# Feature-major GEMMs in split float32: one 512-column product for the weights' high part in place of two of 256

## Chip, cores and metric

The kernel runs on one core of one Trainium2 chip. What counts is the device time of one execution, in microseconds (us).

## The reference

One layer of a bidirectional trunk on 256 tokens of 2048 features, in float32. Every sub-layer has a norm ahead of it and a plain residual add behind it. Cut to what matters:

```python
u = rmsnorm(h, mix_norm)
z, xbc, dt = split(u @ w_in)                     # 2048 -> 4096 + 6144 + 128
xs, B, C = split(silu(dwconv(xbc, 4 taps)))      # 4096 + 1024 + 1024
y = ssd_scan(xs, dt, A, B, C) + flipped scan + xs * d_skip
h = h + (rmsnorm(y * silu(z)) * norm_g) @ w_out  # 4096 -> 2048
q = rmsnorm(h) @ wq;  k, v = split(rmsnorm(mem) @ wkv)
h = h + (softmax(q @ k.T / sqrt(512)) @ v) @ wo  # 4 heads of 512
gate, val = split(rmsnorm(h) @ w_up)             # 2048 -> 2 x 5632
h = h + (silu(dwconv(gate, 3 taps)) * val) @ w_down
return rmsnorm(h) * final_norm
```

## The kernel before

**Split operands.** Each float32 operand of a GEMM is split into a high and a low part of type float32r, and a product is the sum of three: high by high, high by low, low by high. An activation unit holds four tiles of 128 features by 256 tokens, with its high and low parts side by side (`new_unit`). Weights come by DMA as raw tiles of 512 KB into a ring of five (`load_weights`, L119). ScalarE casts a tile to `w_hi` (L106), VectorE subtracts to get `w_lo` (L107); each of these rings has four buffers.

**Three forms of GEMM.** `gemm_feat` (L132), the narrow form here, puts features on the partitions. For each k tile and feature tile it issues three matmuls of 256 columns (L152 to L154), and four feature tiles share one PSUM slot `psg` of two banks. `gemm_feat_wide` (L157), the wide form, is used by the FFN's up projection alone. The high part of the weights meets both parts of the activation in one matmul of 512 columns (L169), the low part meets the high one in 256 columns (L171). A feature tile then takes a whole bank, so that a slot holds two, and its halves are added at the end: a copy on ScalarE (L173) and an add on VectorE (L174). `gemm_tok` (L176) puts tokens on the partitions and stays as it is. There are two slots `psg` and four banks `psm`.

**The SSD stage** goes through eight groups. `project(g)` gives four feature tiles of x and one each of B and C (`bc`); `conv_silu` (L354) multiplies the PSUM bank by 1/rms into a tile `cv_s` (two buffers), then applies the taps into `xs` (two buffers) or `bc`. `project_z(g)` gives `sz` (one buffer). `scan_group(g)` turns x to token-major, works out the decays on ScalarE and VectorE, multiplies by `sz` (L460), and splits the result into a unit (`split_scaled`, L101 and L102). The loop has project(g + 1) ahead of z(g) and scan(g), so that the products of the next group run on TensorE while the scan runs on the other engines:

```python
nxt = project(0)
for g in range(GROUPS):
    cur = nxt
    if g + 1 < GROUPS:
        nxt = project(g + 1)
    sz = project_z(g)
    scan_group(g, *cur, sz)
```

**Behind it**, `residual_units` (L476) adds w_out's and wo's output to the residual stream and splits it again; `query` and `key` split their banks into high and low parts; values, the attention products and the down projection are in the other forms.

**Order.** Tiles wait for buffers of their pool. A planner at build time, with a cost model of its own, fixes the order of instructions on each engine; the engines run in that order, with semaphores between them.

Of the kernel before, what the change touches and what calls it, by code (L numbers as in the profile page):

```python
# [36 lines left out]
def kernel(  # L37
# [28 lines left out]
    def psum_g():  # L66
        """two banks"""
        return sb(ps_g, [P, 2, 512], "psg")
# [16 lines left out]
    # tri[:, 0, l] = 1 where l >= m, tri[:, 1, l] = 1 where l <= m  # L85
# [8 lines left out]
    def new_unit():  # L94
        """4 feature tiles of an operand: high part, low part, and both side by side"""
        both = sb(unit_pool, [P, 4, 2, T], "unit", F32R)
        return both[:, :, 0, :], both[:, :, 1, :], both
# [34 lines left out]
    def gemm_feat(units, wv, cols, k_first=0, first_raw=None):  # L132
        """features on the partitions: banks of two 128-feature tiles by 256 tokens"""
# [23 lines left out]
    def gemm_feat_wide(units, wv, c0, dst):  # L157
        """dst [P, 2, T] = two 128-feature tiles; the high part of the weights meets both parts of the
        operand in one product, so each tile has a bank whose halves add up to it"""
        nk = 4 * len(units)  # L160
        ps = psum_g()
        for k0 in range(0, nk, 4):
            hi, lo = load_weights(wv, k0, [(c0, 2 * P)])
            for kk in range(4):
                kt = k0 + kk
                unit = units[kt // 4]
                for ft in range(2):
                    fs = slice(ft * P, (ft + 1) * P)
                    nc.tensor.matmul(ps[:, ft, :], hi[:, kk, fs], unit[2][:, kt % 4].rearrange("p s t -> p (s t)"),  # L169
                                     start=(kt == 0), stop=False, skip_group_check=True)  # L170
                    nc.tensor.matmul(ps[:, ft, :T], lo[:, kk, fs], unit[0][:, kt % 4, :], start=False,  # L171
                                     stop=(kt == nk - 1), skip_group_check=True)
        nc.scalar.copy(out=dst, in_=ps[:, :, T:])  # L173
        nc.vector.tensor_tensor(out=dst, in0=ps[:, :, :T], in1=dst, op=ALU.add)  # L174

    def gemm_tok(units, wv, c0, k_first=0):  # L176
        """tokens on the partitions: two banks of 128 tokens by 512 features"""
# [23 lines left out]
    def add_square(pool, acc, src2, first):  # L201
        """src2: [P, 2, T]"""
# [7 lines left out]
    def rsqrt_mean(pool, dst, total, n, tags=("rs_v", "rs_s")):  # L210
        """dst = (total / n + eps) ** -0.5: a square root from the table, then one Heron step"""
# [25 lines left out]
    w_in_v = kview(w_in)  # L237
    units_mix = [new_unit() for _ in range(4)]
    with tc.tile_pool(name="xin", bufs=1) as xin:
# [32 lines left out]
        # the column of 1/rms as a row on every partition  # L272
# [12 lines left out]
    with tc.tile_pool(name="ssd", bufs=1) as ssd:  # L285
        acc_y = sb(ssd, [P, 2, T], "acc_y")

# [10 lines left out]
        # log1p(ex) = ln(w) * ex / (w - 1) with w = 1 + ex, and ex itself where w == 1  # L298
# [32 lines left out]
        # decay to the end of the chunk times dt: forward for chunk 0, backward for chunk 1  # L331
# [12 lines left out]
        # exp(cum) where a state comes in: forward rows in chunk 1, backward rows in chunk 0  # L344
# [9 lines left out]
        def conv_silu(banks, f0s, dst):  # L354
            """centred conv of 4 taps over the tokens, bias, silu; two feature tiles per bank"""
            for b, bank in enumerate(banks):
                s = sb(ssd, [P, 2, T], "cv_s", bufs=2)
                nc.vector.tensor_tensor(out=s, in0=two(bank), in1=rows2(r_mix), op=ALU.mult)
                a = dst[:, 2 * b:2 * b + 2, :]
                for j in range(2):  # L360
                    f = f0s[2 * b + j]
                    w = lambda t: pcol("conv_w", f * 4 + t)
                    nc.scalar.activation(out=a[:, j, :], in_=s[:, j, :], func=AF.Identity, scale=w(2), bias=pcol("conv_b", f))
                    for tap, off in ((0, 2), (1, 1)):
                        nc.vector.scalar_tensor_tensor(out=a[:, j, off:], in0=s[:, j, :T - off], scalar=w(tap),
                                                       in1=a[:, j, off:], op0=ALU.mult, op1=ALU.add)
                    nc.vector.scalar_tensor_tensor(out=a[:, j, :T - 1], in0=s[:, j, 1:], scalar=w(3),
                                                   in1=a[:, j, :T - 1], op0=ALU.mult, op1=ALU.add)
                nc.scalar.activation(out=a, in_=a, func=AF.Silu)

        def project(g):
            xs = sb(ssd, [P, 4, T], "xs", bufs=2)
            conv_silu(gemm_feat(units_mix, w_in_v, [(INNER + g * 512, 512)]), [g * 4 + j for j in range(4)], xs)
            bc = sb(ssd, [P, 2, T], "bc", bufs=2)
            conv_silu(gemm_feat(units_mix, w_in_v, [(2 * INNER + g * P, P), (2 * INNER + 1024 + g * P, P)]),
# [3 lines left out]
        def project_z(g):  # L379
            sz = sb(ssd, [P, 4, T], "sz")  # L380
            for b, bank in enumerate(gemm_feat(units_mix, w_in_v, [(g * 512, 512)])):
                nc.vector.tensor_tensor(out=sz[:, 2 * b:2 * b + 2, :], in0=two(bank), in1=rows2(r_mix), op=ALU.mult)
                nc.scalar.activation(out=sz[:, 2 * b:2 * b + 2, :], in_=sz[:, 2 * b:2 * b + 2, :], func=AF.Silu)
# [5 lines left out]
        def scan_group(g, xs, bc, sz):  # L389
# [5 lines left out]
            # token-major x and B  # L395
# [15 lines left out]
            # state that leaves chunk 0 forwards, and the one that leaves chunk 1 backwards  # L411
# [5 lines left out]
            for c in range(2):  # L417
# [8 lines left out]
                # of the two exponents the one of the direction that reaches l from m is <= 0, the other >= 0  # L426
# [14 lines left out]
                # what the incoming state gives, before its decay  # L441
# [34 lines left out]
    def residual_units(pool, hT, banks, u, gname, acc_t, r=None):  # L476
        unit = new_unit()
        for b, bank in enumerate(banks):
            hv = hT[:, u * 4 + 2 * b:u * 4 + 2 * b + 2, :]
            if r is None:  # L480
                nc.vector.tensor_tensor(out=hv, in0=two(bank), in1=hv, op=ALU.add)
            else:
                t = sb(pool, [P, 2, T], "res_t", bufs=2)
                nc.vector.tensor_tensor(out=t, in0=two(bank), in1=rows2(r), op=ALU.mult)
# [35 lines left out]
    with tc.tile_pool(name="res", bufs=1) as res:  # L520
# [4 lines left out]
        with tc.tile_pool(name="att", bufs=1) as att:  # L525
# [4 lines left out]
            for u in range(4):  # L530
                banks = gemm_feat(units_y, w_out_v, [(u * 512, 512)])
                units_xa.append(residual_units(att, hT, banks, u, "g_xa", acc_h, r_ssd))
# [7 lines left out]
            # 1/rms of the queries' tokens as columns: it goes into the scale of the softmax  # L540
# [14 lines left out]

            def query(hd):
                return split_banks(pair("q", [P, 4, T]), gemm_feat(units_xa, wq_v, [(hd * 512, 512)]))

            def key(hd):
                return split_banks(pair("k", [P, 4, T]), gemm_feat(units_mem, wkv_v, [(hd * 512, 512)]))  # L560
# [7 lines left out]
            def three(out_ap, lhsT, rhs, first, last):  # L568
                """one product of operands in two parts each; lhsT, rhs: (hi, lo)"""
# [56 lines left out]
            for u in range(4):  # L626
                banks = gemm_feat(units_o, wo_v, [(u * 512, 512)])
                units_ffn.append(residual_units(att, hT, banks, u, "g_ffn", acc_f))
            inv_rms(att, acc_f, r_ffn, D)

# [126 lines left out]
```

## Time and profile before

| | us |
|---|---|
| median of 3 runs | 1872.16 |
| lowest and highest | 1871.01 and 1872.17 |
| span of the profiled execution, from its first to its last instruction | 1870.4 |
| TensorE busy (share of the span) | 1851.4 (99%) |
| VectorE busy | 1246.3 (67%) |
| ScalarE busy | 1007.2 (54%) |

All rows come from the one profiled execution. PE is TensorE's matmuls, PEld its weight loads, DVE VectorE, ACT ScalarE, SP the engine that issues most DMAs. Matmuls are pipelined and their ends are modelled; the distance from one start to the next is what a matmul costs in a stream.

### The profile page before, as it was taken

The page shows a single profiled execution, that of the slowest core. Times are in us where ns is not written, and L with a number is a line of the kernel's source. Part 1 is how long each engine was busy: PE and PEld are TensorE (multiplying, and loading weights), DVE is VectorE, ACT ScalarE, POOL GpSimd, SP SyncE. Part 2 cuts the span into 40 slices and gives each one's busy share as a digit, 9 for nine tenths or more (in the row PEclk, how much of TensorE's full clock was granted, in tenths as well). Part 3 has the DMA queues.
Part 4 walks back from the last instruction along what each step waited for, and adds up shares of the span by engine and source line. Part 5 has one row for each costly group of instructions (what it writes and reads, how often), then busy time and mean ns, then how long its engine had stood idle before and what let it go on. Part 6 is the DMA issues. An engine that isn't in the chain of part 4 may idle for free.

```text
span 1870.4 us, 31851 instructions
## 1 busy us (share of the span) xinstructions
PE 1851.4 (99%) x12845; PEld 1715.6 (92%) x12845; DVE 1246.3 (67%) x1764; ACT 1007.2 (54%) x1434; POOL 2.3 (0%) x11
## 2 busy tenths in 40 slices
PE   8999999999999999999999999999999999999997
PEld 8999999999999999999999998888888888888886
DVE  7778878988887756554454557666664556666654
ACT  6666767766675544444444446555553345555443
POOL 0000000000000000000000000000000000000000
PEclk9999999999999999999999999999999999999999
DMA  8667666766756655555555556566655565656553
GB/s 288 197 201 214 205 197 195 220 199 183 224 183 223 230 188 181 181 161 178 171 178 172 165 182 202 180 189 188 189 191 194 195 192 185 189 184 189 188 195 113
DMA packets 256947, 359.06 MB, mean 192 GB/s; under 512 B 11616, under 2 KB 145120, under 8 KB 256288
## 3 DMA queue, kind: packets, MB, share of 16 engines
q1 hardware_dynamic: 256720, 356.76, 60.8%
q8 instruction: 100, 1.64, 0.4%
q14 instruction: 47, 0.39, 0.1%
q0 software_dynamic: 80, 0.28, 0.0%
HBM read 352.60 MB, written 4.39 MB: 191 GB/s over the span
## 4 chain that ended last, share of the span: by engine, by line
PE 99%; DMA 0%; DVE 0%; ACT 0%; SPq 0%; issue 0%; DVEq 0%
PE psg L169 18%; PE psg L154 17%; PE psg L152 16%; PE psg L153 16%; PE psg L171 9%; PE psm L190 6%; PE psm L191 6%; PE psm L189 6%; PE psm L449 1%; PE psm L444 1%; PE psm L415 1%; PE psm L572 0%; PE psm L570 0%; PE psm L571 0%; DMA x<-in_x_dram 0%; PE psm L401 0%
## 5 line engine op out<-in xcount | busy, mean ns | idle before, releaser
L107 DVE TENSOR_TENSOR w_lo<-raw,w_hi 128x1024 fp32r<-128x1024 f32 x618 | 753.4, 1223 | 518.4 <-ACT w_hi L106 515.7
L106 ACT CAST w_hi<-raw 128x1024 fp32r<-128x1024 f32 x618 | 645.1, 1048 | 697.7 <-PE psg L153 255.0
L154 PE MATMUL psg<-unit,w_lo 128*128 128x256 f32 x2576 | 733.4, 285 | 0.0
L152 PE MATMUL psg<-unit,w_hi 128*128 128x256 f32 x2576 | 731.6, 284 | 0.0
L153 PE MATMUL psg<-unit,w_hi 128*128 128x256 f32 x2576 | 730.3, 284 | 0.0
L154 PEld LDWEIGHTS psg<-unit,w_lo 128*128 128x128 f32 x2576 | 494.3, 192 | 3.4 <-issue 3.1
L152 PEld LDWEIGHTS psg<-unit,w_hi 128*128 128x128 f32 x2576 | 494.4, 192 | 1.7 <-issue 1.7
L153 PEld LDWEIGHTS psg<-unit,w_hi 128*128 128x128 f32 x2576 | 494.5, 192 | 0.3 <-issue 0.2
L169 PE MATMUL psg<-unit,w_hi 128*128 128x512 f32 x1408 | 493.5, 396 | 0.0
L171 PE MATMUL psg<-unit,w_lo 128*128 128x256 f32 x1408 | 393.2, 279 | 0.0
L169 PEld LDWEIGHTS psg<-unit,w_hi 128*128 128x128 f32 x1408 | 264.3, 188 | 63.6
L171 PEld LDWEIGHTS psg<-unit,w_lo 128*128 128x128 f32 x1408 | 265.2, 188 | 0.1
L189 PE MATMUL psm<-w_hi,unit 128*128 128x512 f32 x480 | 186.8, 389 | 0.0
L190 PE MATMUL psm<-w_lo,unit 128*128 128x512 f32 x480 | 186.8, 389 | 0.0
L191 PE MATMUL psm<-w_hi,unit 128*128 128x512 f32 x480 | 186.8, 389 | 0.0
L189 PEld LDWEIGHTS psm<-w_hi,unit 128*128 128x128 f32 x480 | 90.1, 188 | 18.8
L190 PEld LDWEIGHTS psm<-w_lo,unit 128*128 128x128 f32 x480 | 90.1, 188 | 18.6
L191 PEld LDWEIGHTS psm<-w_hi,unit 128*128 128x128 f32 x480 | 90.1, 188 | 18.5
L431 ACT ACTIVATE r<-r,ncum_tok 128x128 f32<-128x128 f32 x128 | 39.4, 390 | 57.7 <-DMA r<-cum_d 55.1
L432 DVE SCALAR_TENSOR_TENSOR r<-r,ncum_tok 128x128 f32<-128x128 f32 x128 | 36.9, 347 | 17.1 <-ACT r L431 17.1
L437 ACT ACTIVATE t<-cb,dt_tok 128x128 f32<-128x128 f32 x128 | 39.1, 388 | 0.7 <-DVE cb L424 0.2
L438 DVE SCALAR_TENSOR_TENSOR t<-cb,dt_tok,t 128x128 f32<-128x128 f32 x128 | 36.5, 348 | 3.3 <-ACT t L437 3.3
(218 smaller groups left out, 1044.7 us busy)
## 6 DMA issues: line engine op xcount, KB each, us to landing
raw<-in_w_up_dram SPq DMA_DIRECT2D x176, 512.0 KB, 3.6
raw<-in_w_in_dram SPq DMA_DIRECT2D x130, 512.0 KB, 4.6
raw<-in_w_down_dram SPq DMA_DIRECT2D x88, 512.0 KB, 3.6
raw<-in_w_out_dram SPq DMA_DIRECT2D x64, 512.0 KB, 4.3
raw<-in_wkv_dram SPq DMA_DIRECT2D x64, 512.0 KB, 3.7
raw<-in_w_in_dram SPq DMA_DIRECT2D x64, 256.0 KB, 4.5
r<-cum_d SPq DMA_DIRECT2D x16, 1024.0 KB, 6.3
raw<-in_wq_dram SPq DMA_DIRECT2D x32, 512.0 KB, 3.6
```

What stands on the lines that cost most here:

```text
L106: nc.scalar.copy(out=hi, in_=src)
L107: nc.vector.tensor_tensor(out=lo, in0=src, in1=hi.bitcast(F32), op=ALU.subtract)
L152: nc.tensor.matmul(dst, wh, uh, start=first, stop=False, skip_group_check=True)
L153: nc.tensor.matmul(dst, wh, ul, start=False, stop=False, skip_group_check=True)
L154: nc.tensor.matmul(dst, wl, uh, start=False, stop=last, skip_group_check=True)
L169: nc.tensor.matmul(ps[:, ft, :], hi[:, kk, fs], unit[2][:, kt % 4].rearrange("p s t -> p (s t)"), start=(kt == 0), stop=False, skip_group_ ...
L171: nc.tensor.matmul(ps[:, ft, :T], lo[:, kk, fs], unit[0][:, kt % 4, :], start=False, stop=(kt == nk - 1), skip_group_check=True)
L189: nc.tensor.matmul(banks[tt], uh, hi[:, kk, :], start=(kt == 0), stop=False)
L190: nc.tensor.matmul(banks[tt], uh, lo[:, kk, :], start=False, stop=False)
L191: nc.tensor.matmul(banks[tt], ul, hi[:, kk, :], start=False, stop=(kt == nk - 1))
L431: nc.scalar.activation(out=t1[:, h, :], in_=t1[:, h, :], func=AF.Identity, bias=ncum_tok[:, c, hf:hf + 1])
L437: nc.scalar.activation(out=t2[:, h, :], in_=cb[:, 1, :], func=AF.Copy, scale=dt_tok[:, c, hb:hb + 1])
```

## The change

`gemm_feat_wide` takes lists of columns, as `gemm_feat` does, and returns its PSUM slot; `add_halves` does the copy and the add. All callers of `gemm_feat` but the one for dt now go through 256 columns at a time with the wide form: `project`, `project_z`, `residual_units` (w_out and wo), `query` and `key`. Where nothing is multiplied in between (wo), the two halves are added to the residual stream one after the other.

```diff
-    def gemm_feat_wide(units, wv, c0, dst):
+    def gemm_feat_wide(units, wv, cols):
         nk = 4 * len(units)
         ps = psum_g()
         for k0 in range(0, nk, 4):
-            hi, lo = load_weights(wv, k0, [(c0, 2 * P)])
+            hi, lo = load_weights(wv, k0, cols)
...
+        return ps
+
+    def add_halves(dst, ps):
         nc.scalar.copy(out=dst, in_=ps[:, :, T:])
         nc.vector.tensor_tensor(out=dst, in0=ps[:, :, :T], in1=dst, op=ALU.add)
...
-        def conv_silu(banks, f0s, dst):
-            for b, bank in enumerate(banks):
-                s = sb(ssd, [P, 2, T], "cv_s", bufs=2)
-                nc.vector.tensor_tensor(out=s, in0=two(bank), in1=rows2(r_mix), op=ALU.mult)
...
+        def conv_silu(ps, f0s, a):
+            s = sb(ssd, [P, 2, T], "cv_s", bufs=2)
+            add_halves(s, ps)
+            nc.vector.tensor_tensor(out=s, in0=s, in1=rows2(r_mix), op=ALU.mult)
...
         def project(g):
             xs = sb(ssd, [P, 4, T], "xs", bufs=2)
-            conv_silu(gemm_feat(units_mix, w_in_v, [(INNER + g * 512, 512)]), [g * 4 + j for j in range(4)], xs)
+            for b in range(2):
+                conv_silu(gemm_feat_wide(units_mix, w_in_v, [(INNER + g * 512 + b * 256, 256)]),
+                          [g * 4 + 2 * b, g * 4 + 2 * b + 1], xs[:, 2 * b:2 * b + 2, :])
             bc = sb(ssd, [P, 2, T], "bc", bufs=2)
-            conv_silu(gemm_feat(units_mix, w_in_v, [(2 * INNER + g * P, P), (2 * INNER + 1024 + g * P, P)]),
+            conv_silu(gemm_feat_wide(units_mix, w_in_v, [(2 * INNER + g * P, P), (2 * INNER + 1024 + g * P, P)]),
                       [32 + g, 40 + g], bc)
...
         def project_z(g):
             sz = sb(ssd, [P, 4, T], "sz")
-            for b, bank in enumerate(gemm_feat(units_mix, w_in_v, [(g * 512, 512)])):
-                nc.vector.tensor_tensor(out=sz[:, 2 * b:2 * b + 2, :], in0=two(bank), in1=rows2(r_mix), op=ALU.mult)
-                nc.scalar.activation(out=sz[:, 2 * b:2 * b + 2, :], in_=sz[:, 2 * b:2 * b + 2, :], func=AF.Silu)
+            for b in range(2):
+                z = sz[:, 2 * b:2 * b + 2, :]
+                add_halves(z, gemm_feat_wide(units_mix, w_in_v, [(g * 512 + b * 256, 256)]))
+                nc.vector.tensor_tensor(out=z, in0=z, in1=rows2(r_mix), op=ALU.mult)
+                nc.scalar.activation(out=z, in_=z, func=AF.Silu)
...
-    def residual_units(pool, hT, banks, u, gname, acc_t, r=None):
+    def residual_units(pool, hT, units, wv, u, gname, acc_t, r=None):
         unit = new_unit()
-        for b, bank in enumerate(banks):
+        for b in range(2):
+            ps = gemm_feat_wide(units, wv, [(u * 512 + b * 256, 256)])
             hv = hT[:, u * 4 + 2 * b:u * 4 + 2 * b + 2, :]
             if r is None:
-                nc.vector.tensor_tensor(out=hv, in0=two(bank), in1=hv, op=ALU.add)
+                nc.vector.tensor_tensor(out=hv, in0=ps[:, :, T:], in1=hv, op=ALU.add)
+                nc.vector.tensor_tensor(out=hv, in0=ps[:, :, :T], in1=hv, op=ALU.add)
             else:
                 t = sb(pool, [P, 2, T], "res_t", bufs=2)
-                nc.vector.tensor_tensor(out=t, in0=two(bank), in1=rows2(r), op=ALU.mult)
+                add_halves(t, ps)
+                nc.vector.tensor_tensor(out=t, in0=t, in1=rows2(r), op=ALU.mult)
...
+            def split_wide(dst, units, wv, c0):
+                for b in range(2):
+                    t = sb(att, [P, 2, T], "res_t", bufs=2)
+                    add_halves(t, gemm_feat_wide(units, wv, [(c0 + b * 256, 256)]))
+                    split_plain(dst[0][:, 2 * b:2 * b + 2, :], dst[1][:, 2 * b:2 * b + 2, :], t)
+                return dst
...
             def query(hd):
-                return split_banks(pair("q", [P, 4, T]), gemm_feat(units_xa, wq_v, [(hd * 512, 512)]))
+                return split_wide(pair("q", [P, 4, T]), units_xa, wq_v, hd * 512)
...
             def key(hd):
-                return split_banks(pair("k", [P, 4, T]), gemm_feat(units_mem, wkv_v, [(hd * 512, 512)]))
+                return split_wide(pair("k", [P, 4, T]), units_mem, wkv_v, hd * 512)
```

## Rows read from the trace of the kernel before

**Rows 1.** The page: busy us by engine; granted clock in tenths, 40 slices.

```profile
PE 1851.4 (99%) x12845; PEld 1715.6 (92%) x12845; DVE 1246.3 (67%) x1764; ACT 1007.2 (54%) x1434; POOL 2.3 (0%) x11
...
PEclk9999999999999999999999999999999999999999
```

**Rows 2.** The chain that ended last, shares of the span by line.

```profile
by line: PE psg L169 17.5%; PE psg L154 16.6%; PE psg L152 16.5%; PE psg L153 16.5%; PE psg L171 8.8%; PE psm L190 5.8%; PE psm L191 5.8%; PE psm L189 5.8%; PE psm L449 0.9%; PE psm L444 0.8%; PE psm L415 0.7%; PE psm L572 0.4%; PE psm L570
```

**Rows 3.** The page, costliest groups: count | busy us, mean ns | idle us.

```profile
L152 PE MATMUL psg<-unit,w_hi 128*128 128x256 f32 x2576 | 731.6, 284 | 0.0
...
L169 PE MATMUL psg<-unit,w_hi 128*128 128x512 f32 x1408 | 493.5, 396 | 0.0
```

**Rows 4.** Timeline of TensorE in w_out: start us, length us, engine, line.

```profile
645.85 0.28 PE L152 MATMUL psg<-unit,w_hi 128*128 128x256 f32 x1
...
652.33 0.28 PE L152 MATMUL psg<-unit,w_hi 128*128 128x256 f32 x1
```

**Rows 5.** Timeline of TensorE, the FFN's first half.

```profile
1299.95 0.40 PE L169 MATMUL psg<-unit,w_hi 128*128 128x512 f32 x1
...
1306.19 0.40 PE L169 MATMUL psg<-unit,w_hi 128*128 128x512 f32 x1
```

**Rows 6.** Timeline of TensorE, the FFN's second half.

```profile
1599.72 0.40 PE L169 MATMUL psg<-unit,w_hi 128*128 128x512 f32 x1
...
1606.08 0.40 PE L169 MATMUL psg<-unit,w_hi 128*128 128x512 f32 x1
```

**Rows 7.** Windows: length, busy us of PE, PEld, DVE, ACT, POOL; clock, DMA share.

```profile
180.00:245.00 65.00, 65.00 (x549) 63.43 (x548) 55.06 (x101) 44.98 (x78) 0.00 (x0) 1.00 0.66 203
640.00:740.00 100.00, 100.00 (x836) 100.00 (x835) 61.47 (x75) 49.09 (x63) 0.00 (x0) 1.00 0.57 189
```

**Rows 8.** Groups of VectorE by line and form, columns as in rows 3.

```profile
L174 DVE TENSOR_TENSOR f_s<-psg,f_s 128x512 f32<-128x512 f32 x44 | 30.1, 684 | 0.0
...
L358 DVE TENSOR_TENSOR cv_s<-psg,r_mix 128x512 f32<-128x512 f32 x24 | 15.7, 682 | 0.0
```

**Rows 9.** Groups of ScalarE by line and form.

```profile
L173 ACT COPY f_s<-psg 128x512 f32<-128x512 f32 x44 | 25.6, 582 | 0.6 <-DVE r_ffn L221 0.6
```

**Rows 10.** Timeline of VectorE through one group, with repeats (x) merged.

```profile
210.55 1.28 DVE L358 TENSOR_TENSOR cv_s<-psg,r_mix 128x512 f32<-128x512 f32 x2
...
222.07 1.67 DVE L102 SCALAR_TENSOR_TENSOR unit<-xs,par,unit 128x256 fp32r<-128x256 f32 x4
...
231.96 1.66 DVE L367 SCALAR_TENSOR_TENSOR xs<-cv_s,par,xs 128x255 f32<-128x255 f32 x4
...
234.68 0.68 DVE L358 TENSOR_TENSOR cv_s<-psg,r_mix 128x512 f32<-128x512 f32 x1
```

**Rows 11.** Timeline of ScalarE in the same group.

```profile
224.53 2.08 ACT L363 ACTIVATE xs<-cv_s,par 128x256 f32<-128x256 f32 x4
```

**Rows 12.** The chain in order of time, where two scans begin: start us.

```profile
180.13 0.87 PE psm L401 x8
...
245.15 0.87 PE psm L401 x8
```

**Rows 13.** Timeline of VectorE at the end of the SSD stage.

```profile
541.79 1.28 DVE L460 TENSOR_TENSOR xs<-xs,sz 128x512 f32<-128x512 f32 x2
...
544.57 1.28 DVE L382 TENSOR_TENSOR sz<-psg,r_mix 128x512 f32<-128x512 f32 x2
...
584.20 1.67 DVE L102 SCALAR_TENSOR_TENSOR unit<-xs,par,unit 128x256 fp32r<-128x256 f32 x4
```

**Rows 14.** Timeline of TensorE where z(7) ends and w_out begins.

```profile
535.19 0.28 PE L153 MATMUL psg<-unit,w_hi 128*128 128x256 f32 x1
...
537.49 0.36 PE L154 MATMUL psg<-unit,w_lo 128*128 128x256 f32 x1
```

**Rows 15.** DMA issues: tiles, queue, count, KB each, median us to landing.

```profile
raw<-in_w_up_dram SPq DMA_DIRECT2D x176, 512.0 KB, 3.6
raw<-in_w_in_dram SPq DMA_DIRECT2D x130, 512.0 KB, 4.6
```

More of the change, by code (lines that the diff above doesn't have):

```diff
@@ L352 @@
         nc.vector.tensor_copy(out=dx_tok.rearrange("p c h -> p (c h)"), in_=ps[:, :P])
-        def conv_silu(banks, f0s, dst):
-            for b, bank in enumerate(banks):
-                s = sb(ssd, [P, 2, T], "cv_s", bufs=2)
-                nc.vector.tensor_tensor(out=s, in0=two(bank), in1=rows2(r_mix), op=ALU.mult)
[L359 to L369, printed above, removed]
+        def conv_silu(ps, f0s, a):
+            s = sb(ssd, [P, 2, T], "cv_s", bufs=2)
+            add_halves(s, ps)
+            nc.vector.tensor_tensor(out=s, in0=s, in1=rows2(r_mix), op=ALU.mult)
+            for j in range(2):
+                f = f0s[j]
+                w = lambda t: pcol("conv_w", f * 4 + t)
+                nc.scalar.activation(out=a[:, j, :], in_=s[:, j, :], func=AF.Identity, scale=w(2), bias=pcol("conv_b", f))
+                for tap, off in ((0, 2), (1, 1)):
+                    nc.vector.scalar_tensor_tensor(out=a[:, j, off:], in0=s[:, j, :T - off], scalar=w(tap),
+                                                   in1=a[:, j, off:], op0=ALU.mult, op1=ALU.add)
+                nc.vector.scalar_tensor_tensor(out=a[:, j, :T - 1], in0=s[:, j, 1:], scalar=w(3),
+                                               in1=a[:, j, :T - 1], op0=ALU.mult, op1=ALU.add)
+            nc.scalar.activation(out=a, in_=a, func=AF.Silu)
@@ L530 @@
             for u in range(4):
-                banks = gemm_feat(units_y, w_out_v, [(u * 512, 512)])
-                units_xa.append(residual_units(att, hT, banks, u, "g_xa", acc_h, r_ssd))
+                units_xa.append(residual_units(att, hT, units_y, w_out_v, u, "g_xa", acc_h, r_ssd))
             inv_rms(att, acc_h, r_xa, D)
@@ L626 @@
             for u in range(4):
-                banks = gemm_feat(units_o, wo_v, [(u * 512, 512)])
-                units_ffn.append(residual_units(att, hT, banks, u, "g_ffn", acc_f))
+                units_ffn.append(residual_units(att, hT, units_o, wo_v, u, "g_ffn", acc_f))
             inv_rms(att, acc_f, r_ffn, D)
@@ L642, in ffn_unit @@
                     s = sb(ffn, [P, 2, T], "f_s", bufs=2)
-                    gemm_feat_wide(units_ffn, w_up_v, i * 512 + b * 256, s)
+                    add_halves(s, gemm_feat_wide(units_ffn, w_up_v, [(i * 512 + b * 256, 256)]))
                     nc.vector.tensor_tensor(out=s, in0=s, in1=rows2(r_ffn), op=ALU.mult)
@@ L659, in ffn_unit @@
                     s = sb(ffn, [P, 2, T], "f_s", bufs=2)
-                    gemm_feat_wide(units_ffn, w_up_v, FFN + i * 512 + b * 256, s)
+                    add_halves(s, gemm_feat_wide(units_ffn, w_up_v, [(FFN + i * 512 + b * 256, 256)]))
                     nc.vector.tensor_tensor(out=s, in0=s, in1=rows2(r_ffn), op=ALU.mult)
```

## Prediction, before the change was run

> **What bounds the kernel now.** I read the page first. TensorE is busy 99% of the span, and its clock stands at the upper level, 2.4 GHz, in all forty slices [rows 1]; VectorE follows with 67%. The chain that ended last shows what that 99% is made of: 49.6% lies on the three lines of the narrow form (L152 to L154), 26.3% on the two of the wide form (L169, L171), 17.4% on the token-major products, which stay [rows 2]. So time is won by what the matmuls cost each other, and lost wherever TensorE comes to stand.
>
> Busy times of TensorE overlap (a matmul of 256 columns is listed with 284 ns [rows 3]), so I took the price from starts. I call a pair one k tile by one feature tile: three products in the narrow form, two in the wide one, 768 columns in both. In the timeline of w_out, 18 narrow pairs take 652.33 - 645.85 = 6.48 us, 360 ns each, 120 ns a matmul [rows 4]. In the first half of the FFN, 18 wide pairs take 6.24 us, 347 ns each [rows 5]; in its second half 6.36 us, 353 ns each [rows 6]. The wide form thus runs in two rhythms. 768 columns at 2.4 GHz are 320 ns. What is left is 3 x 13.3 ns in the narrow form and 2 x 13.3 ns in the quicker wide rhythm: I read it as a fixed price per matmul (my reading of three paces, not a row). The slower rhythm gives back half a price.
>
> The windows show the slack. In one group of the SSD stage VectorE is busy 55.06 of 65 us and ScalarE 44.98; in w_out only 61.47 and 49.09 of 100 [rows 7].
>
> **The change part by part.** *Products.* L152 stands 2576 times [rows 3]; 16 of these are the dt product, which keeps its form. 2560 pairs change: 8 x 10 x 16 = 1280 in the SSD stage, 16 x 32 = 512 in w_out, 3 x 256 in queries, keys and wo. Each loses one weight load and one matmul start. The bounds are 360 - 353 = 7 ns and 360 - 347 = 13 ns, in all 17 and 34 us. The chain's shares give 0.496 x 1870.4 / 2576 = 360 ns against 0.263 x 1870.4 / 1408 = 349 ns [rows 2, 3], the mean over both rhythms with their starts. Which rhythm the new stretches fall into I can't tell, so I take 10 ns: **25.6 us off**, half of it in the SSD stage. The untouched FFN may change its rhythm too: its later 640 pairs x 7 ns, 4 us either way.
>
> The Trainium skill ("TensorE: Matmul & The Clock Gate", Back-to-back issue gap) gives an isolated warm matmul N / 2.4 plus 2.5 ns. By that rule a pair would cost 327.5 ns narrow and 325 ns wide, and the change would save 2.5 ns x 2560 = 6 us before any loss. The rows above disagree with it in both forms.
>
> *Read-out.* A block is now two feature tiles in two halves. There are 40 + 8 + 8 + 8 + 8 = 72 blocks, the number of bank read-outs of before. Each gets one more VectorE add, 684 ns by L174 [rows 8], 49 us in all, and each but the eight of wo one more ScalarE copy, 582 ns by L173 [rows 9], 37 us. The multiplication by 1/rms keeps its price (682 ns from PSUM at L358 [rows 8]). Outside the SSD stage the idle third of VectorE and half of ScalarE hide all that: zero. In the SSD stage a group has five blocks: VectorE gets 3.4 us and stands at 58.5 of about 63.4 us (65 less 160 x 10 ns), 92%; ScalarE at 47.9. There the cover is thin: both queues run in order, so an add that waits for its copy holds up the w_lo splits behind it, and those hold TensorE.
>
> *Loads.* As many weight tiles as before, 512 KB each, but the wide w_in, w_out, wq, wkv-key and wo tiles now come in rows of 1 KB. w_up already does: it lands in 3.6 us, w_in with mostly longer rows in 4.6 us [rows 15]. Five raw tiles of 2.8 us of matmul time each cover that. Zero; I exclude a gain because TensorE doesn't wait for loads now.
>
> *PSUM slots.* This is where I expect something back. Two slots stay, but each is now filled in 32 pairs, 11.2 us, instead of 23.0 us, and a slot is free only when its block has been copied and added, which needs the tile that takes the result.
>
> First place: bc. conv_silu takes its input tile cv_s from two buffers; xs uses both, so bc is read only when the first xs block has gone through its taps. Those wait for the xs buffer, which the scan gives back with its last split. In the trace: the splits L102 start at 222.07, the scaled copies L363 at 224.53, the last taps L367 at 231.96, and only then, at 234.68, L358 reads bc [rows 10, 11]. bc itself was complete about 64 x 0.36 = 23.0 us before the next scan starts at 245.15, so at 222.1 [rows 12]. Its slot is free 13.3 us after it is full. Today nobody needs it sooner, for z fills the other slot for 23.0 us. After the change z's first block takes 11.2 us and its second needs bc's slot: a stall of 13.3 - 11.2 = 2.1 us, and with the copy ahead of the add and bc done a little earlier up to 3.6. It is less where the first xs block's taps run ahead of the second's (by up to half of the 9 us from L363 to the end of L367, no stall left), and the transposes of the next scan can move into it. Bounds 0 and 3.6 us in the six groups that have it, 0 and 22 us; I take 1 us each, **6 us**.
>
> Second place: the last group. sz has one buffer, and scan(6) gives it back with L460 at 541.79 [rows 13]. z(7) is complete at about 535.3, then TensorE goes on with w_out at 537.49 in the other slot [rows 14]. After the change z's two blocks hold both slots, and the first can't be read before L460: 541.79 + 1.3 + 0.58 + 0.68 = 544.4. w_out waits from 537.5 to 544.4, less what scan(7)'s own products fill of it (I take 1.5 us): **5.5 us**, bounds 0 (if the scan moves up as z is delayed no further) and 7. From there w_out has 2 blocks x 28 k tiles x 2 = 112 pairs, 39 us, which reach to 583.5 even with nothing between them; scan(7)'s products come between, and the last unit is split from 584.20 [rows 13]. That about reaches; zero.
>
> Sum against the profiled span: 1870.4 - 25.6 + 6 + 5.5 = 1856. The median of the runs, 1872.2, stands 1.8 us above that span, which I carry over: **1858 us**.
>
> **The rivals.** *Nothing stalls.* The planner puts the reads early, and scans fill what gaps there are. For it: VectorE is idle 10 of 65 us in a group [rows 7], and L358 read xs at 210.55, right as it was complete [rows 10]. Against it: the two tiles cv_s and sz, which no order of instructions gets round. Time: 1872.2 - 25.6 = 1847, down to 1838 if the quick rhythm holds throughout.
>
> *Columns set the pace.* If only streamed columns counted, 768 against 768 would give nothing, and only the losses stay: 1872 without them, 1872.2 + 11.5 = 1884 with them. Against it: the same chip in the same run holds 360 ns in one form and 347 to 353 ns in the other [rows 4 to 6]. The Trainium skill's rule above, with 6 us off, comes out near this rival.
>
> *The SSD stage turns to VectorE, and the kernel gets slower.* With 92% of VectorE taken, z's second block waits for bc's slot in every group, and the late adds push back the w_lo splits and with them the next scan. The point from which it decides: the 25.6 us less the 5.5 at the end are gone when each of the six groups loses 3.4 us. For it: the bound of 3.6 us from the trace, and a VectorE with 5 us left in a group in place of 10. Against it: w_out, attention and wo have no such coupling and save 13 us by themselves. At 5 us a group: 1872.2 - 25.6 + 30 + 5.5 = 1882; between 3 and 5 us, 1870 to 1882.
>
> **How the numbers follow.** Forecast, a gain partly given back, 0.55: its own range is 1848 to 1867 (rhythm 17 to 34 us, 10 to 11.5 lost). No stall 0.20, columns 0.05, slower SSD stage 0.20. A measurement of this kernel tells about 0.2%, 3.7 us, from no change. Faster: 0.52 of the forecast and all of the first rival, 0.72. Same: 0.03 of the forecast, 0.02 of the second, 0.05 of the third, 0.10. Slower: 0.03 and 0.15, 0.18. The time is the forecast's, 1858. The range from 1842 to 1876 leaves out the quick end of the first rival (0.05), half of the second (0.03) and the upper part of the third (0.10).
>
> **What would show it.** Right: L152 to L154 shrink to the 16 dt pairs, the wide lines carry 3968 pairs at 347 to 353 ns between starts, the stretch from w_out to wo is 9 to 17 us shorter, TensorE shows gaps ahead of z's second block in groups 1 to 6 and one of some 5 us where w_out begins; one scan starts 63 to 65 us after the other. Wrong: pairs at 360 ns or at 325 ns; no gap at these two places; scans over 66 us apart; or waits of TensorE for w_lo, which I price only inside the bounds above.

## The result: slower by 1.3%, and the profile after

The changed kernel takes **1896.44 us** (median of 4 runs, 1892.20 to 1899.49) against 1872.02 before (also four runs): a ratio of **1.0128, 95% interval 1.0113 to 1.0143**. The forecast was 1858, and the range ended at 1876.

The profiled run took 1898.0 us with a span of 1896.2. The page shows where to look: busy us by engine, then the span in 40 slices, TensorE's busy tenths and its granted clock.

```profile
PE 1838.1 (97%) x10285; PEld 1583.9 (84%) x10285; DVE 1292.2 (68%) x1836; ACT 1041.4 (55%) x1498; POOL 2.3 (0%) x11
...
PE   8999999999978899999999999999999999999997
...
PEclk9999999999989899999999999999999999999999
...
L169 PE MATMUL psg<-unit,w_hi 128*128 128x512 f32 x3968 | 1399.9, 397 | 18.8 <-DVE sz L178 8.4
L171 PE MATMUL psg<-unit,w_lo 128*128 128x256 f32 x3968 | 1115.7, 281 | 0.8 <-DVE w_lo L107 0.8
```

TensorE is busy 13.3 us less than before, with 2560 matmuls fewer [rows 1], and yet the span is 25.8 us longer: 39.1 us more in which it stands. That time is not spread. It lies in the twelfth to fourteenth slice, 521 to 664 us, and there the clock drops too, which stood at 9 in all forty slices before [rows 1]. The second last line tells more: ahead of 512-column products TensorE stood 18.8 us, 8.4 of them until an add into `sz` was done, while the products with `w_lo` waited 0.8 us.

The view of waits, TensorE, whole span: what it waited for, us in total, times, longest.

```profile
PE psm L525 <- ACT junk L511: 11.8, 1, 11.8
PE psg L169 <- DVE sz L178: 8.4, 2, 4.6
PE psg L169 <- DVE cv_s L178: 6.4, 5, 1.7
PE psm L422 <- ACT b_tok L417: 5.6, 1, 5.6
```

**The products are as forecast.** 3968 pairs stand on the two wide lines. The timeline of w_out, where [rows 4] read 360 ns a pair:

```profile
645.85 0.40 PE L169 MATMUL psg<-unit,w_hi 128*128 128x512 f32 x1
...
652.21 0.40 PE L169 MATMUL psg<-unit,w_hi 128*128 128x512 f32 x1
```

Eighteen pairs in 6.36 us, 353 ns. Over each stage, from start to start and without the stretches at the lower clock, a pair takes 349.4 ns in the SSD stage, 352.8 in w_out, 349.0 from queries to wo: 1280 x 10.6 + 512 x 7.2 + 768 x 11.0 ns = 25.7 us saved.

**So the losses are 25.8 + 25.7 = 51.5 us of span.** Intervals of over 0.7 us from one of TensorE's starts to the next, added up, give 12.6 us in the groups (116 to 506 us), 14.3 around the last scan (506 to 600), 16.5 at the memory tokens (600 to 632) and 3.8 ahead of the groups (from 30 us on); behind 632 us there are none. Before, there was one from 30 us on, of 1.7 us.

*The groups.* The predicted place, with the predicted chain. The timelines of VectorE, ScalarE and TensorE in one group:

```profile
227.98 1.67 DVE L102 SCALAR_TENSOR_TENSOR unit<-xs,par,unit 128x256 fp32r<-128x256 f32 x4
...
237.86 1.66 DVE L370 SCALAR_TENSOR_TENSOR xs<-cv_s,par,xs 128x255 f32<-128x255 f32 x4
...
241.24 0.69 DVE L178 TENSOR_TENSOR cv_s<-psg,cv_s 128x512 f32<-128x512 f32 x1 [0.59 <-ACT cv_s L177]
```
```profile
229.74 2.08 ACT L366 ACTIVATE xs<-cv_s,par 128x256 f32<-128x256 f32 x4
...
240.64 0.57 ACT L177 COPY cv_s<-psg 128x512 f32<-128x512 f32 x1
```
```profile
239.85 0.82 PE L408 MATMUL psm<-ident,xs 128*128 128x128 f32 x6
```

The last split of the scan, the scaled copies, the taps, and only then the copy and the add that empty bc's slot at 241.9. The transposes of the next scan fill part of the stall; what is left is an interval of 1.0 to 2.0 us in each of five groups. The sixth, in group 1 at 169.8 us, takes 4.8 us and ends with an add into `sz`. It isn't the tile that is late there. The scan ahead was done with `sz` at 160.5, but the add stands behind taps of x on VectorE's queue (L368 and L370, from 167.25 to 172.8), as the read of bc does in the other groups:

```profile
159.23 1.28 DVE L467 TENSOR_TENSOR xs<-xs,sz 128x512 f32<-128x512 f32 x2
...
173.86 0.69 DVE L178 TENSOR_TENSOR sz<-psg,sz 128x512 f32<-128x512 f32 x1
```

*The last scan.* `sz` comes free with L467 (L460 of the kernel before), which starts at 550.56 and not at 541.79 [rows 13]; the add that reads z(7) starts at 557.37. VectorE, TensorE and ScalarE:

```profile
550.56 1.28 DVE L467 TENSOR_TENSOR xs<-xs,sz 128x512 f32<-128x512 f32 x2
...
557.37 1.28 DVE L178 TENSOR_TENSOR sz<-psg,sz 128x512 f32<-128x512 f32 x2
```
```profile
548.68 3.77 PE L422 MATMUL psm<-xsd,b_tok 128*128 128x512 f32 x4 [5.61 <-ACT b_tok L417]
...
558.10 0.79 PE L169 MATMUL psg<-unit,w_hi 128*128 128x512 f32 x1 [3.82 <-DVE sz L178]
```
```profile
547.39 0.98 ACT L438 ACTIVATE r<-r,ncum_tok 128x128 f32<-128x128 f32 x3 [3.86 <-DMA r<-cum_d]
548.28 0.35 ACT L417 COPY b_tok<-psm 128x256 f32<-128x256 f32 x1
```

Behind the wait for `b_tok` is a DMA: on ScalarE the copy into `b_tok` stands behind L438, which waits 3.86 us for `r`. On VectorE, L439 waits 2.57 us for L438 at 547.82 and stands ahead of L467.

*The memory tokens.* Here the prediction had nothing. TensorE, ScalarE and VectorE:

```profile
609.35 0.28 PE L171 MATMUL psg<-unit,w_lo 128*128 128x256 f32 x1
621.43 1.09 PE L525 MATMUL psm<-ident,mem 128*128 128x128 f32 x4 [11.80 <-ACT junk L511]
...
631.61 0.50 PE L169 MATMUL psg<-unit,w_hi 128*128 128x512 f32 x1 [1.46 <-DVE res_t L178]
```
```profile
615.11 0.63 ACT L511 ACTIVATE junk<-mem 128x512 f32<-128x512 f32 x1 [4.51 <-DMA mem<-in_mem_dram]
...
630.25 1.07 ACT L177 COPY res_t<-psg 128x512 f32<-128x512 f32 x2
```

Between the scans and attention the memory tokens are loaded, normed and transposed (L503 to L527), in memory that the SSD stage gives up with its last instruction (`r_ssd`, done at 608.0; the load is issued at 608.10). w_out's read-out needs `res_t`, which lies in memory that the memory tokens give up in turn. So no block of w_out can be read before about 630. In the trace of before the same read came no sooner, on VectorE:

```profile
631.40 1.28 DVE L484 TENSOR_TENSOR res_t<-psg,r_ssd 128x512 f32<-128x512 f32 x2
```

But there the two slots held 2 x 4 feature tiles x 32 k tiles = 256 pairs, 92 us of matmuls from 537.5 on, enough to last until then. Now they hold 128 pairs, 45 us. They are used up at 609.5.

*The clock.* Windows of the changed kernel: the four stretches between 30 us and the last product in which the clock was at its lower level of 1.2 GHz. The figure behind TensorE's busy time and count is the granted clock, 0.50 of 2.4 GHz:

```profile
173.42:180.25 6.83, 5.65 (x17) 0.50 0.45 133
545.47:552.30 6.83, 3.62 (x5) 0.50 0.77 245
555.71:562.54 6.83, 4.44 (x14) 0.50 0.00 0
613.74:627.39 13.65, 4.12 (x17) 0.50 0.36 133
```

Each begins within one of the four longest intervals and reaches beyond its end: behind 558.10 the first pair takes 810 ns and the next ones 640. TensorE is busy 17.8 us in these stretches. At 2.4 GHz the same work would take about half of that, so the lower clock cost some 9 us (an estimate from these four rows). The transposes of the memory tokens, which took 4.1 us before, take 6.5 here.

Busy time should have shrunk by the 25.7 us of the products and shrank by 13.3. Of the 12.4 us between them some 9 are the clock; the rest isn't broken down. With the 39.1 us in which TensorE stands they make up the 51.5.

### The profile page after: what moved, and what is told of

It is laid out like the page before. It is cut to its first block, busy times and chain, and to the rows that moved or that the text cites. A ratio compares the mean times of both kernels' runs of the same rounds, so it can differ in the third digit from the quotient of the medians.

```text
span 1896.2 us, 26903 instructions
## 1 busy us (share of the span) xinstructions
PE 1838.1 (97%) x10285; PEld 1583.9 (84%) x10285; DVE 1292.2 (68%) x1836; ACT 1041.4 (55%) x1498; POOL 2.3 (0%) x11
## 4 chain that ended last, share of the span: by engine, by line
PE 91%; DVE 4%; DMA 2%; issue 1%; ACT 1%; SPq 0%; DVEq 0%; ACTq 0%
PE psg L169 46%; PE psg L171 23%; PE psm L194 6%; PE psm L193 6%; PE psm L195 6%; DVE w_lo L107 1%; DVE xs L368 1%; PE psm L422 1%; PE psm L456 1%; PE psm L451 1%; DVE unit L102 1%; DMA r<-cum_d 0%; PE psm L586 0%; PE psm L588 0%; DMA x<-in_x_dram 0%
## 5 line engine op out<-in xcount | busy, mean ns | idle before, releaser
L169 PE MATMUL psg<-unit,w_hi 128*128 128x512 f32 x3968 | 1399.9, 397 | 18.8 <-DVE sz L178 8.4
L169 PEld LDWEIGHTS psg<-unit,w_hi 128*128 128x128 f32 x3968 | 746.3, 188 | 193.6 <-issue 9.3
L171 PEld LDWEIGHTS psg<-unit,w_lo 128*128 128x128 f32 x3968 | 751.6, 189 | 2.8 <-issue 1.3
L195 PEld LDWEIGHTS psm<-w_hi,unit 128*128 128x128 f32 x480 | 90.1, 188 | 18.8
L438 ACT ACTIVATE r<-r,ncum_tok 128x128 f32<-128x128 f32 x128 | 39.9, 390 | 37.1 <-DMA r<-cum_d 34.5
L439 DVE SCALAR_TENSOR_TENSOR r<-r,ncum_tok 128x128 f32<-128x128 f32 x128 | 37.9, 345 | 14.7 <-ACT r L438 14.5
L445 DVE SCALAR_TENSOR_TENSOR t<-cb,dt_tok,t 128x128 f32<-128x128 f32 x128 | 36.4, 346 | 0.5 <-ACT t L444 0.5
L178 DVE TENSOR_TENSOR f_s<-psg,f_s 128x512 f32<-128x512 f32 x44 | 30.1, 684 | 0.0
L368 DVE SCALAR_TENSOR_TENSOR xs<-cv_s,par,xs 128x254 f32<-128x254 f32 (+1 forms) x64 | 26.8, 476 | 0.2 <-ACT xs L366 0.2
L177 ACT COPY f_s<-psg 128x512 f32<-128x512 f32 x44 | 25.5, 580 | 0.2 <-DVE r_ffn L225 0.2
L664 ACT ACTIVATE f_a<-f_s,par 128x256 f32<-128x256 f32 x44 | 24.0, 593 | 0.1
L422 PE MATMUL psm<-xsd,b_tok 128*128 128x512 f32 x32 | 17.1, 655 | 5.6 <-ACT b_tok L417 5.6
L459 DVE SCALAR_TENSOR_TENSOR xs<-xs,par,psm 128x128 f32<-128x128 f32 x64 | 17.9, 342 | 5.4 <-PE psm L456 5.3
```

The costliest lines, as they stand in the source:

```text
L195: nc.tensor.matmul(banks[tt], ul, hi[:, kk, :], start=False, stop=(kt == nk - 1))
L438: nc.scalar.activation(out=t1[:, h, :], in_=t1[:, h, :], func=AF.Identity, bias=ncum_tok[:, c, hf:hf + 1])
L439: nc.vector.scalar_tensor_tensor(out=t1[:, h, :], in0=r[:, 1, h, :], scalar=ncum_tok[:, c, hb:hb + 1], in1=t1[:, h, :], op0=ALU.add, op1=A ...
L445: nc.vector.scalar_tensor_tensor(out=t2[:, h, :], in0=cb[:, 0, :], scalar=dt_tok[:, c, hf:hf + 1], in1=t2[:, h, :], op0=ALU.mult, op1=ALU.add)
```

## The experiments

**The theory:** a slot that holds two feature tiles in place of four gives TensorE half the work to bridge a late read-out; three tiles are late (cv_s, sz, res_t), and that costs the 50 us, whatever form the products have. **The rivals:** the read-out's copies and adds load VectorE and ScalarE in the SSD stage; or the form is worth nothing.

**1. Half the slot, nothing else.** The kernel before with its narrow form, but 256 columns at a time, no copy, no added add:

```diff
-            conv_silu(gemm_feat(units_mix, w_in_v, [(INNER + g * 512, 512)]), [g * 4 + j for j in range(4)], xs)
+            for hb in range(2):
+                conv_silu(gemm_feat(units_mix, w_in_v, [(INNER + g * 512 + hb * 256, 256)]),
+                          [g * 4 + 2 * hb, g * 4 + 2 * hb + 1], xs[:, 2 * hb:2 * hb + 2, :])
```

and the like for z, w_out, wo, queries and keys.

> The kernel before, narrow form and its read-outs kept, but every feature-major product taken 256 columns at a time, so that a PSUM slot holds two feature tiles in one bank instead of four in two. Slot theory (the loss comes from slots that hold half the work while cv_s, sz and res_t are late): 1905 to 1920 us, with TensorE idle in the SSD groups, behind z(7) and ahead of 632 us as in the changed kernel, here without the gain per pair. Read-out theory (the loss comes from the added copies and adds on ScalarE and VectorE): 1870 to 1877 us, for none are added.

Measured: 1902.64 us (1900.47 to 1905.14), ratio 1.0168, interval 1.0151 to 1.0185: 2 us below the slot theory's range, and far from the other. Its waits, TensorE, columns as above:

```profile
PE psm L519 <- ACT junk L505: 10.0, 1, 10.0
PE psg L152 <- DVE sz L385: 7.9, 1, 7.9
```

The two large gaps are back at the same places, in the old form. The slots cost 30.6 us by themselves; the groups lose only 2 us here. The weight tiles also come in rows of 1 KB, as in the changed kernel, but none of TensorE's waits in this run is for them.

**2. The read-out, nothing else.** The kernel before with a copy and a second operation on VectorE (a maximum of equal values) ahead of the multiplication, in `conv_silu`, z and w_out:

```diff
-                nc.vector.tensor_tensor(out=s, in0=two(bank), in1=rows2(r_mix), op=ALU.mult)
+                nc.scalar.copy(out=s, in_=two(bank))
+                nc.vector.tensor_tensor(out=s, in0=two(bank), in1=s, op=ALU.max)
+                nc.vector.tensor_tensor(out=s, in0=s, in1=rows2(r_mix), op=ALU.mult)
```

> The kernel before with the added read-out work alone: in the SSD stage and behind w_out each bank is copied on ScalarE and then joined with its copy on VectorE (maximum of equal values, so nothing else changes), then multiplied from SBUF. Form and slots stay. Slot theory: 1870 to 1877 us, the cover of four feature tiles per slot hides it. Read-out theory: over 1885 us, VectorE some 58 of 65 us busy in a group and TensorE waiting.

Measured: 1879.37 us (1878.08 to 1880.19), ratio 1.0039, interval 1.0024 to 1.0054. Between the two expectations: 7 us, most of it in intervals of 6.3 us in the groups, where scan products wait for VectorE (`t` L445, 4.5 us in all, 1.5 of them behind the groups, where the kernel before had 1.4). The read-out is not free, as the prediction's sum had it, but it is the smaller part.

**3. res_t in memory of its own.** The changed kernel with `res_t` in a pool that is there from the start; one of five raw tiles goes to make room:

```diff
-    ring_raw = ctx.enter_context(tc.tile_pool(name="ring_raw", bufs=5))
+    ring_raw = ctx.enter_context(tc.tile_pool(name="ring_raw", bufs=4))
...
-                t = sb(pool, [P, 2, T], "res_t", bufs=2)
+                t = sb(const, [P, 2, T], "res_t0", bufs=2)
```

> The changed kernel with the tile res_t of w_out's read-out in memory of its own (not laid over that of the memory tokens), paid for by four raw weight tiles instead of five. Slot theory: the idle 16.5 us ahead of 632 us go, and 1874 to 1886 us are left; the gaps in the groups and behind z(7) stay. Read-out theory: 1892 to 1899 us, no change, since the same copies and adds are done.

**4. The control for it:** four raw tiles alone.

> The changed kernel with four raw weight tiles instead of five and nothing else: the price of the memory that the runs rt and half4 took. Slot theory: no change, 1890 to 1900 us, for ScalarE's casts don't wait for loads. If it is faster by some us, that much of rt's and half4's gain came from another order of the planner and not from the tiles.

Measured: 1873.70 us with `res_t` moved (10 runs, 1872.27 to 1875.32; ratio 1.0009, interval 1.0000 to 1.0019), 1892.82 us for the control (1886.77 to 1895.12; ratio 1.0094, interval 1.0074 to 1.0113). By the medians this one tile is worth 19.1 us, by the two ratios 16: the control's four runs lie 8 us apart. The intervals at the memory tokens, 16.9 us in the control, go; whether the slow matmuls behind them add to it is within the spread. The run with `res_t` moved comes out just below the slot theory's range, the control within it. In the waits of the run with `res_t` moved nothing of the memory tokens is left. The groups' `cv_s` stays with 3.9 us, and so does the last scan:

```profile
PE psg L169 <- DVE sz L178: 6.4, 2, 3.6
PE psm L422 <- ACT b_tok L417: 6.3, 1, 6.3
```

**5. A second sz.** The control with `sz` twice:

```diff
-            sz = sb(ssd, [P, 4, T], "sz")
+            sz = sb(ssd, [P, 4, T], "sz", bufs=2)
```

> The changed kernel with two buffers of sz, on four raw tiles. Slot theory: the gaps at z(1) (4.8 us) and behind z(7) (11 us) go, but w_out then fills its two slots earlier and waits longer for res_t, 20 to 28 us instead of 16.5, so that 1880 to 1890 us are left. If the gaps were independent of each other, all 16 us would be gained: 1876 to 1881 us, with the gap ahead of res_t as it was.

Measured: 1891.72 us (1889.96 to 1894.91), ratio 1.0100, interval 1.0085 to 1.0116. Neither expectation held: no change against the control. The gap at the last scan is gone, and the next one is larger. The one in group 1 stays, with 4.5 us, though there are two `sz` now, so it doesn't wait for that buffer.

```profile
PE psm L525 <- ACT junk L511: 18.3, 1, 18.3
```

It was 11.5 in the control. w_out starts sooner, uses up its two slots sooner, and waits for the same memory tokens. A gap removed ahead of a stop that stays moves into that stop.

**6. Four tiles for all read-outs.** The control with one pool of four tiles, there from the start, for `conv_silu`, z, w_out, queries and keys:

```diff
-            s = sb(ssd, [P, 2, T], "cv_s", bufs=2)
+            s = sb(const, [P, 2, T], "half", bufs=4)
...
-                add_halves(z, gemm_feat_wide(units_mix, w_in_v, [(g * 512 + b * 256, 256)]))
-                nc.vector.tensor_tensor(out=z, in0=z, in1=rows2(r_mix), op=ALU.mult)
+                s = sb(const, [P, 2, T], "half", bufs=4)
+                add_halves(s, gemm_feat_wide(units_mix, w_in_v, [(g * 512 + b * 256, 256)]))
+                nc.vector.tensor_tensor(out=z, in0=s, in1=rows2(r_mix), op=ALU.mult)
```

> The changed kernel with one set of four read-out tiles, in memory of its own, shared by conv_silu, z and w_out to wo in place of cv_s, sz and res_t as targets of the copy and the add; four raw weight tiles instead of five. Slot theory: a slot is free as soon as TensorE has filled it and the two engines come round, all three gaps shrink to a few us together, 1848 to 1862 us. Read-out theory: no gain, over 1885 us.

Measured: 1864.92 us (1863.22 to 1866.03), ratio 0.9961, interval 0.9946 to 0.9976: 27.9 us off the control by the medians (25 by the ratios), and faster than before, but 3 us above the slot theory's range. What is left is mostly the work that covers the last unit of the SSD stage, which the prediction's second place set at zero. The longest waits, but for the load of x at the start:

```profile
PE psg L169 <- DVE unit L102: 3.8, 1, 3.8
PE psg L171 <- DVE w_lo L107: 3.6, 5, 1.1
```

**7. More work ahead of that unit.** The same, with w_out's first four feature tiles in the narrow form, so that the one slot holds 128 pairs, 46 us of work, of which 112 can run before that unit is there:

```diff
+        first = r is not None and u == 0
+        banks = gemm_feat(units, wv, [(u * 512, 512)]) if first else None
```

> The run half4 with the first four feature tiles of w_out in the narrow form, four to a slot. Slot theory: TensorE then has 112 + 56 pairs to run until the last group's unit is split, in place of 112, and the last gaps of half4 between 565 and 594 us (some 6 to 10 us) shrink; 128 pairs cost 10 ns more, 1.3 us: 1857 to 1862 us. If the gaps come from the scan itself and not from the cover: 1864 to 1868 us.

Measured: 1857.52 us (1856.56 to 1858.44), ratio 0.9916, interval 0.9901 to 0.9931. As expected: the intervals between 506 and 600 us shrink from 11.4 to 4.3 us.

**8. The order of the products.** Experiment 6 again, but in each k tile both products of 512 columns first, then both of 256:

```diff
                                      start=(kt == 0), stop=False, skip_group_check=True)
+                for ft in range(2):
+                    fs = slice(ft * P, (ft + 1) * P)
                     nc.tensor.matmul(ps[:, ft, :T], lo[:, kk, fs]
```

> The run half4 with another order of products in the wide form: for each k tile the two of 512 columns, then the two of 256. If the slower rhythm (353 in place of 347 ns a pair) comes from the change between long and short products, all pairs go at 347 ns or less and 1852 to 1858 us result. If a short product needs a long one ahead of it to hide its weight load, the two short ones cost 120 ns each and the pair 351 ns everywhere: 1862 to 1870 us.

Measured: 1859.16 us (1857.36 to 1859.99), ratio 0.9923, interval 0.9909 to 0.9938. That lies between the two expectations, and so does the pace: the two rhythms of the FFN become one of 348.3 ns. Over all wide pairs the mean goes from 349.3 to 348.4 ns, which is 3.5 of the 5.8 us between this run and experiment 6; the rest isn't broken down.

**9. The same order in the changed kernel as it is,** without any added tile:

> The changed kernel with one edit: within a k tile the two products of 512 columns come first, then the two of 256. No buffer is added. Theory (the order sets the rhythm of the wide pairs, the slots set the gaps, and the two are independent): pairs at 348.3 ns everywhere, so 3968 x about 1 to 2 ns off, and the gaps between 500 and 632 us stay at about 30 us and a little longer since the products that lie ahead of them are shorter; 1889 to 1896 us. Rival (the order also moves when a slot comes free): gaps differ by over 5 us from those of the changed kernel.

Measured: 1911.78 us (1909.27 to 1912.71), ratio 1.0208, interval 1.0192 to 1.0223. The theory's number was missed by 16 us; the rival was right. The pairs do run at 348.3 ns in the FFN, but the groups now have six intervals of 3.3 to 5.6 us, 25.2 us in all, in place of 12.6. First the wait for bc's slot over the whole span, then one window over a group of this run, and behind it the same window of the changed kernel:

```profile
PE psg L169 <- DVE cv_s L180: 19.8, 5, 5.3
```
```profile
375.00:440.00 65.00, 59.69 (x354) 50.94 (x353) 55.00 (x100) 44.95 (x81) 0.00 (x0) 0.95 0.65 192
```
```profile
375.00:440.00 65.00, 63.64 (x388) 54.58 (x387) 57.77 (x107) 47.15 (x84) 0.00 (x0) 1.00 0.71 203
```

The intervals stand 68 to 71 us apart, where the changed kernel's stand 65 apart, and behind them the granted clock is lower. VectorE is busy less of the window, not more, so a fuller VectorE isn't the reason. My reading, which no run tests, is that the quicker products come sooner to a read-out that the scan's work holds up. Why that read-out then comes later itself, so that a group becomes longer than 65 us, isn't settled.

**10. z and w_out narrow, no tile added.** The changed kernel with the wide form for x, B, C, queries, keys and wo alone:

```diff
-            for b in range(2):
+            for b, bank in enumerate(gemm_feat(units_mix, w_in_v, [(g * 512, 512)])):
                 z = sz[:, 2 * b:2 * b + 2, :]
-                add_halves(z, gemm_feat_wide(units_mix, w_in_v, [(g * 512 + b * 256, 256)]))
-                nc.vector.tensor_tensor(out=z, in0=z, in1=rows2(r_mix), op=ALU.mult)
+                nc.vector.tensor_tensor(out=z, in0=two(bank), in1=rows2(r_mix), op=ALU.mult)
```

and the like in `residual_units` for w_out.

> The changed kernel with only z and w_out back in the narrow form (four feature tiles in a slot); x, B, C, queries, keys and wo stay wide, and no buffer is added. 768 pairs in the SSD stage and 768 in attention and wo keep the saving of 10 ns, 15.4 us. Theory (slots of half the work do harm only where the tile that takes the result comes late: sz at the end of the scans, res_t until the memory tokens are done): both seams have their 23 us slots again, so the gaps between 500 and 632 us are gone, and what stays lost is a few us in the groups; 1857 to 1865 us. Rival (the read-out's extra copies and adds in the SSD stage cost the time): three of five blocks of a group still carry them, so more than half of the loss stays; 1875 us or more.

Measured: 1864.39 us (1861.82 to 1864.70), ratio 0.9954, interval 0.9939 to 0.9968. The theory's range, at its upper end. The large slots are back where a tile is late, and of TensorE's waits in the groups and behind them the two longest are:

```profile
PE psm L455 <- DVE t L446: 1.5, 1, 1.5
PE psg L154 <- DVE w_lo L107: 0.6, 1, 0.6
```

Three of five blocks of a group carry the longer read-out here, so the read-out load can't have been the main cause.

**11. All of it.** Experiments 6, 7 and 8 together:

> The version that the runs so far point to: the changed kernel with four shared tiles for the read-outs (one raw tile less), the 512-column products of a k tile ahead of the 256-column ones, and w_out's first four feature tiles in the narrow form. Theory (three separate gains: tiles free in time, one rhythm of 348 ns, cover for the last unit of the SSD stage): the two single edits took 5.8 and 7.4 us off the version with four tiles, and the 16 k tiles that go back to the narrow form give back nothing more here; together 1851 to 1856 us. Rival (both edits remove the same gap, or the shorter products open it again): no better than the better of the two, 1856 to 1859 us.

Measured: **1849.31 us** (1848.48 to 1850.48), ratio 0.9875, interval 0.9858 to 0.9891, below both expectations and 47 us below the change as made. (The two single gains, taken off experiment 6, give 1851.8.) The window from 506 to 632 us, where the changed kernel had TensorE busy 100.65 of 126 us at a clock of 0.89:

```profile
506.00:632.00 126.00, 122.45 (x870) 112.07 (x869) 102.14 (x185) 82.40 (x153) 0.00 (x0) 0.99 0.66 207
```

## Why the prediction was wrong

**Products: right.** 25.6 us forecast, 25.7 measured, inside the bounds of 17 to 34. Which rhythm a new stretch takes was left open, and both occur; that they mix to the 10 ns in the middle is luck. The rival that columns alone set the pace is out: the narrow form's 360 ns is nowhere kept. The rule of the Trainium skill ("TensorE: Matmul & The Clock Gate", Back-to-back issue gap) is for an isolated matmul, and the page says that a stream with weight loads is spaced otherwise. Applied to the stream, as the prediction did, it gives an estimate of 325 ns for a wide pair; no stretch here is under 346.

**Read-out: too low.** It was set at zero on the strength of idle shares, 92% of VectorE in the groups included. Experiment 2 measures 7 us. TensorE hardly waits for `w_lo` in the changed kernel (0.8 us); the read-outs delay the scan and the emptying of slots.

**First place: right chain, too small.** Six groups of 1 us were forecast; five intervals of 1.0 to 2.0 us came, 7.8 us in all, each partly filled by the scan's transposes. The sixth, in group 1, took 4.8 us, over the bound of 3.6: there z's first block, and not bc, stands behind the taps. 12.6 us came in all where 6 were forecast.

**Second place: the term that was mis-sized.** 5.5 us forecast with bounds 0 and 7; 14.3 us of intervals came between 506 and 600 us. I worked from the time of L460 in the trace of before, 541.79, as though that scan stayed where it was. In the changed kernel that multiplication starts 8.8 us later, at 550.56. In groups 0 to 5 it is already 4.6 to 5.8 us late, from the first group on and without growing; the rest comes at the end, where it stands behind work on the late `r` of the last scan, and TensorE stands 5.6 us for `b_tok` for the same reason. And the copy out of z(7) did not follow it at once, as my sum had it: `sz` was free at 551.8, but ScalarE came to that copy at 556.0 and VectorE to the add at 557.4. An upper bound for a seam has to move with what is lost ahead of it, and has to count what stands ahead of the read-out in its engines' queues.

**The step that failed: "That about reaches; zero."** I had counted what w_out's two slots hold, and asked only whether that reaches to the last unit of y. I did not ask when the first of these slots can be *read*. Its target `res_t` is in memory that the memory tokens give up at about 630 us, 20 us after the slots are used up. That cost 16.5 us of intervals, and moving the tile took 16 to 19 us off (experiments 3 and 4): the largest single loss, and absent from the sum. The trace of before had it in plain sight, in a read of `res_t` at 631.40 for products that began at 537.5. What I did compare didn't hold either once the other stop was gone: experiments 6 and 7 show some 7 us at the last unit.

**The clock: absent from the sum.** Priced as idle time alone, the gaps would be worth 39 us; some 9 more went into matmuls at the lower level. The trace of before has no interval over 1.7 us from 30 us on, and from there to its last product its clock stayed at the upper level.

**The rivals.** The one for a slower kernel had the right sign and the wrong place: it put the loss into the groups, at 3.4 to 5 us each, where five of the six lost 1.0 to 2.0 us. Only with the order of experiment 9 do the groups come into that rival's range. "Nothing stalls", 1838 to 1847, is the time of a kernel with the read-out tiles free: experiment 11 comes near it with 1849.

The terms as measured: 30.6 us for the slots (experiment 1), 7 for the read-out (experiment 2), 25.7 saved. That sums to 1884, and 1896 was measured: some 12 us come only when both meet. That a longer read-out empties small slots later would explain it, but wasn't measured by itself. That the seams are not independent is shown (experiment 5).

## What to carry to other kernels

When a change makes a PSUM slot hold less work, go to each place where the reader of a slot is late and compare two times: when the slots are used up, and when the tile that takes the read-out comes free, including tiles whose memory another stage still holds. Late reads that cost nothing before are in the trace; list them by how long after its products each read comes. Sum such gaps from front to back, since one that is closed reappears at the next stop that stays. The Trainium skill ("Perfetto Trace Analysis", Optimization Strategy) says that the same gap repeated on the engine that should be saturated can mean too little SBUF or PSUM for the next tile; the gaps of the groups agree: with four shared tiles (experiment 6) they went from 10.7 us in the control to 3.3. The dearest gaps here, though, were single ones.

## What the runs showed of the hardware

- The wide pair has two rhythms, 347 and 353 ns, and the order of products changes the pace: alternating 512 and 256 columns gives either, from stretch to stretch; two of 512 and then two of 256 gave 348.3 ns throughout the FFN (experiments 8, 9 and 11). A fixed price for each matmul, my reading of three paces, doesn't explain that, and nothing here does.
- A gap can cost more than its length. In the changed kernel the four intervals of 4.1 to 12.1 us that begin at 169.8, 542.8, 554.0 and 609.4 us came with 34.1 us at the lower of the two levels, in which pairs started 640 ns apart in place of 350. Intervals of 3.3 to 5.6 us once a group brought the granted clock of the groups to 0.95 to 0.99 (experiment 9); those of 1 to 2 us in the changed kernel's groups left it at 1.00. The length alone doesn't tell: where TensorE was idle for 2.1 us at 594 us in experiment 6, 3.4 us at the lower level followed, and where it was idle for 2.8 us at 171 us in experiment 3, none did.
